# Four DRAM reads of each turn moved from the sync queue to ACT's queue in a two-layer decoder trunk

## The chip, the cores and the metric

One Trainium2 chip, one core. The metric is the device time of one execution of the program in microseconds (us). In the rows that follow, PE is the matmul engine (PEld its weight loads), DVE, ACT and POOL are the vector, scalar and general engines, and SP is the engine that issues most DMAs. An entry such as SPq or ACTq is a DMA issue on that engine's queue. L186 is line 186 of the kernel.

## What is computed

A trunk of two decoder layers over 256 positions of width 2048, all in float32. Cut to what matters:

```
for l in range(2):
    h = rmsnorm(x, attn_norm[l])
    z = h @ w_in[l]                     # q, k, v of four head groups, 4 heads x 128 each
    mixed = concat(fox(z), moba(z), diff(z), stick_breaking(z))
    x = x + mixed @ w_out[l]
    h = rmsnorm(x, ffn_norm[l])
    act = silu(h @ w_gate[l]) * (h @ w_up[l])        # width 5632
    x = x + act @ w_down[l]
return rmsnorm(x, final_norm)
```

## The kernel before

**Weights.** All weights are streamed once, in 784 blocks of 128 x 1024 numbers (512 KB). `load(b)` (L186, on SP) brings a block into one of four `raw` buffers. `split_parts` makes of it a rounded half `hi` on ACT (L195) and the rest `lo` on DVE (L196), each with three buffers. PE then multiplies a block by the activations with three products (hi by hi, hi by lo, lo by hi), twelve matmuls for each block (L356 to L358 in the projections, L374 in the gate and up products).

**The order of the work** is written out by hand: instructions stand on each engine's queue in the order in which the code issues them, and a queue doesn't overtake. For each block `run_ahead` issues the load of a block some way ahead, then `hi` and `lo` of the block three ahead of PE; then come the twelve matmuls, and then `tick()`, which moves three lists of generators (`evacs`, `background`, `spare`) one step on. So a generator's `yield` means: the next step stands one block later in every queue. Buffers tie the stream together: a `raw` buffer comes free when `lo` of its block is done, so `load` waits on DVE; a `hi` buffer comes free when PE is done with its block, so `hi` waits on PE.

**The turn.** Activations come out of PE with positions on the partitions; the next stage wants channels there. `turn_steps` (L379 to L397) does that through DRAM. DVE transposes 32 x 32 squares into `tr` (L384); one step later SP writes `tr` to the DRAM tile `mem` (L387); two steps later four reads of 128 KB each bring `mem` back with its parts rearranged (L393), each into 32 partitions, either into a tile `back` or straight into a `q` or `k` tile; two steps after that the consumer stands. There are 50 turns: 16 of q or k of the head groups, 22 of the FFN's activations (`act_steps`, L896 on ACT and L897 on DVE read `back`), and 12 of output columns (`add_turned`): four after each layer's output projection, and four after the first layer's down projection. In `add_turned`, DVE adds `back` to the residual `x_all` (L833); ACT and DVE make the next stage's operand `xh` of it (L299, L300), from which PE goes on. In a turn of q or k, ACT copies `back` (L429), or PE reads the tile itself (L612 and others).

Of the kernel before, what the change touches and what calls it, by code (L numbers as in the profile page):

```python
# [167 lines left out]
def trunk(ctx: ExitStack, tc: tile.TileContext, x_t, vec, w, consts, fin, y):  # L168
    nc = tc.nc
# [209 lines left out]
    def turn_steps(get, back=None):  # L379


        tr = tp.tile([P, 2, GC], F32, name="tr", tag="tr", bufs=1)
        for t in range(2):
            V.transpose(tr[:, t], get(t))  # L384
        yield
        mem = dr.tile([2, 4, 32, 4, P], F32, name="mem", tag="mem")
        nc.sync.dma_start(mem.rearrange("t i r g n -> (i r) t (g n)"), tr)  # L387
        yield
        yield
        if back is None:  # L390
            back = tp.tile([P, 8, 4, 32], F32, name="back", tag="back", bufs=1)
        for g in range(4):
            nc.sync.dma_start(back[32 * g:32 * g + 32].rearrange("r a k n -> r a (k n)"),  # L393
                              mem[:, :, :, g].rearrange("t i r n -> r (t i) n"))
        yield
        yield
        return back.rearrange("p a k n -> p k a n")  # L397
# [7 lines left out]
    def q_or_k_steps(name, which, outs, to, ready):  # L405

        z = tp.tile([P, 2, GC], F32, name="z", tag="g", bufs=1)
        if name in TABLES:
            at, n = TABLES[name]
            halves_of = lambda a: a.rearrange("p (s h n) -> p s h n", h=2, n=n)  # L410
            ms = tp.tile([P, 2, GC], F32, name="ms", tag="tr", bufs=1)
            for m, out in enumerate((z, ms)):
                for t in range(2):
                    tab = con[:, at + (2 * m + t) * n:at + (2 * m + t) * n + n]
                    V.scalar_tensor_tensor(out[:, t].rearrange("p (s n) -> p s n", n=n),
                                           outs[t].rearrange("p (s n) -> p s n", n=n), state["rcol"][:, t:t + 1],
                                           tab[:, None, :].to_broadcast([P, GC // n, n]), op0=ALU.mult, op1=ALU.mult)
            yield
            zh, mh = (a.rearrange("p t (s h n) -> p (t s) h n", h=2, n=n) for a in (z, ms))
            V.tensor_tensor(zh[:, :, 0], zh[:, :, 0], mh[:, :, 1], op=ALU.subtract)  # L420
            V.tensor_tensor(zh[:, :, 1], zh[:, :, 1], mh[:, :, 0], op=ALU.add)
        else:
            r = state["rq" if which == "q" else "rcol"]
            for t in range(2):
                A.activation(z[:, t], outs[t], AF.Copy, scale=r[:, t:t + 1])
        yield
        if which == STATIONARY[name]:
            new = yield from turn_steps(lambda t: z[:, t])
            A.activation(to.rearrange("p h (a n) -> p h a n", n=32), new, AF.Copy)  # L429
            yield  # L430
        else:
            yield from turn_steps(lambda t: z[:, t], to.rearrange("p h s -> p (h s)").rearrange("p (a h n) -> p a h n", h=NH, n=32))
        ready[which] = True
# [395 lines left out]
    def add_turned(n, outs, gain):  # L829

        new = yield from turn_steps(lambda t: outs[t])
        of = x_all[:, 4 * n:4 * n + 4].rearrange("p k (a n) -> p k a n", n=32)
        V.tensor_tensor(of, of, new, op=ALU.add)  # L833
        for j in range(4 * n, 4 * n + 4):
            halves_of_x(j, gain(j))
            square_sum(j)
            if j % 2:
                yield
# [168 lines left out]
```

## Time and profile before

| what | value |
| --- | --- |
| median of 3 runs | 2247.93 us |
| the runs | 2247.28 to 2248.83 us |
| the profiled execution | 2248.83 us |
| its span in the trace | 2247.0 us |
| mean granted TensorE clock | 0.996 of full speed |
| PE busy | 2223.6 us, 99% of the span |
| DVE busy | 1301.0 us, 58% |
| ACT busy | 1054.6 us, 47% |
| the sync queue's packets | 66.2% of the time of the 16 DMA engines |

The span is what the trace shows from the first instruction to the last; the profiled execution is 1.8 us longer, and itself 0.9 us above the median. Busy times leave out DMA issues, which the timeline shows as entries of SPq and ACTq. A timeline's row gives start, duration, engine, line, operation, output and inputs, the number of instructions run together, and in brackets the idle time just ahead of it with what ended it.

### The profile page before, as it was taken

The numbers are of one execution on the slowest core, as the hardware profiler recorded it, in microseconds if no ns is written. First come the engines' busy times: TensorE is split into PE (matmuls) and PEld (weight loads), VectorE is DVE, ScalarE is ACT, GpSimd is POOL, SyncE is SP. The second block draws the span as 40 slices with busy tenths as digits, with TensorE's granted clock in tenths as the row PEclk, the third lists the DMA queues.
The fourth block names the chain that finished last, engine by engine and source line by source line (L and its number), as shares of the span: only waits on it lengthen the run. The fifth ranks groups of instructions, "written<-read, shape, count | busy, mean of one in ns | idle before, by whom it ended". The sixth has DMA issues, their size and how long they took to land.

```text
span 2247.0 us, 26619 instructions
## 1 busy us (share of the span) xinstructions
PE 2223.6 (99%) x9977; PEld 1832.2 (82%) x9977; DVE 1301.0 (58%) x1442; ACT 1054.6 (47%) x1296; POOL 195.8 (9%) x189
## 2 busy tenths in 40 slices
PE   9999999999999999999999999999999999999997
PEld 6888888788888888888878888878888888888886
DVE  6768655655555555455566776566555555554444
ACT  6454644544444444444444556445444444444443
POOL 2019200100000000000000290011000000000000
PEclk9999999999999999999999999999999999999999
DMA  7766556777667667666657565567777776676664
GB/s 256 225 206 203 181 188 206 231 223 216 215 217 227 209 212 226 213 207 206 209 196 232 191 203 188 183 214 228 226 223 237 250 231 211 224 223 199 201 196 147
DMA packets 190497, 476.42 MB, mean 212 GB/s; under 512 B 17440, under 2 KB 72992, under 8 KB 190368
## 3 DMA queue, kind: packets, MB, share of 16 engines
q1 hardware_dynamic: 189792, 473.93, 66.2%
q8 instruction: 78, 1.28, 0.2%
q10 hardware_dynamic: 576, 0.79, 0.1%
q14 instruction: 51, 0.42, 0.1%
HBM read 444.24 MB, written 30.41 MB: 211 GB/s over the span
## 4 chain that ended last, share of the span: by engine, by line
PE 89%; DMA 4%; DVE 3%; ACT 2%; issue 1%; SPq 1%; ACTq 0%; DVEq 0%
PE gate L374 20%; PE up L374 20%; PE po L356 9%; PE po L358 9%; PE po L357 9%; PE in L356 7%; PE in L357 7%; PE in L358 7%; DMA back<-mem 2%; DMA mem<-tr 2%; DVE lo L196 1%; ACT hi L195 1%; SPq L393 0%; DVE x_all L833 0%; DVE tr L384 0%
## 5 line engine op out<-in xcount | busy, mean ns | idle before, releaser
L196 DVE TENSOR_TENSOR lo<-raw,hi 128x1024 fp32r<-128x1024 f32 (+1 forms) x785 | 961.2, 1227 | 880.1 <-ACT hi L195 879.6
L195 ACT ACTIVATE hi<-raw 128x1024 fp32r<-128x1024 f32 (+1 forms) x785 | 829.6, 1059 | 1080.3 <-PE up L374 487.4
L374 PE MATMUL gate<-hi,xh 128*128 128x512 f32 x1408 | 548.2, 389 | 0.5 <-ACT hi L195 0.5
L374 PE MATMUL up<-hi,xh 128*128 128x512 f32 x1408 | 547.8, 389 | 0.0
L374 PEld LDWEIGHTS gate<-hi,xh 128*128 128x128 f32 x1408 | 264.3, 188 | 56.0 <-ACT hi L195 1.2
L374 PEld LDWEIGHTS up<-hi,xh 128*128 128x128 f32 x1408 | 264.4, 188 | 54.8
L356 PE MATMUL in<-hi,xh 128*128 128x512 f32 x768 | 304.7, 397 | 4.1 <-ACT hi L195 2.3
L357 PE MATMUL in<-lo,xh 128*128 128x512 f32 x768 | 301.5, 393 | 1.4 <-DVE lo L196 1.3
L358 PE MATMUL in<-hi,xh 128*128 128x512 f32 x768 | 301.0, 392 | 0.0
L374 PE MATMUL gate<-lo,xh 128*128 128x512 f32 x704 | 274.5, 390 | 1.1 <-DVE lo L196 1.1
L374 PE MATMUL up<-lo,xh 128*128 128x512 f32 x704 | 273.9, 389 | 0.0
L356 PE MATMUL po<-hi,act 128*128 128x512 f32 x704 | 273.9, 389 | 0.0
L357 PE MATMUL po<-lo,act 128*128 128x512 f32 x704 | 273.9, 389 | 0.0
L358 PE MATMUL po<-hi,act 128*128 128x512 f32 x704 | 273.9, 389 | 0.0
L356 PEld LDWEIGHTS in<-hi,xh 128*128 128x128 f32 x768 | 145.4, 189 | 34.9 <-ACT hi L195 3.4
L357 PEld LDWEIGHTS in<-lo,xh 128*128 128x128 f32 x768 | 145.3, 189 | 32.5 <-DVE lo L196 3.3
L358 PEld LDWEIGHTS in<-hi,xh 128*128 128x128 f32 x768 | 145.3, 189 | 30.7
L374 PEld LDWEIGHTS gate<-lo,xh 128*128 128x128 f32 x704 | 132.1, 188 | 30.6 <-DVE lo L196 3.4
L358 PEld LDWEIGHTS po<-hi,act 128*128 128x128 f32 x704 | 132.2, 188 | 27.5
L357 PEld LDWEIGHTS po<-lo,act 128*128 128x128 f32 x704 | 132.2, 188 | 27.4
L356 PEld LDWEIGHTS po<-hi,act 128*128 128x128 f32 x704 | 132.2, 188 | 27.4
L374 PEld LDWEIGHTS up<-lo,xh 128*128 128x128 f32 x704 | 132.2, 188 | 27.2
(206 smaller groups left out, 1473.8 us busy)
## 6 DMA issues: line engine op xcount, KB each, us to landing
raw<-w SPq DMA_DIRECT2D x783, 512.0 KB, 4.3
mem<-tr SPq DMA_DIRECT2D x50, 512.0 KB, 4.3
back<-mem SPq DMA_DIRECT2D x168, 128.0 KB, 4.8
k<-mem SPq DMA_DIRECT2D x24, 128.0 KB, 4.2
memb<-trb SPq DMA_DIRECT2D x16, 128.0 KB, 3.8
x_all<-memb SPq DMA_DIRECT2D x4, 512.0 KB, 6.2
x_all<-x_t SPq DMA_DIRECT2D x7, 256.0 KB, 7.1
q<-mem SPq DMA_DIRECT2D x8, 128.0 KB, 4.7
```

Of the source, the lines that this page charges most:

```text
L195: A.activation(hi[:, c], raw[:, c], AF.Copy)
L196: V.tensor_tensor(lo[:, c], raw[:, c], hi[:, c].bitcast(F32), op=ALU.subtract)
L356: T.matmul(outs[t], xlo, wh, start=first, stop=False)
L357: T.matmul(outs[t], xhi, wl, start=False, stop=False)
L358: T.matmul(outs[t], xhi, wh, start=False, stop=last)
L374: T.matmul(outs[n][t], st, wt[:, n * GC:(n + 1) * GC], start=first, stop=last)
```

## The change

The four reads of `turn_steps` are issued by ACT (`nc.scalar`) and no more by SP (`nc.sync`). Where they stand among the steps, and the waits that they carry, are what they were.

```diff
@@ -390,7 +390,7 @@
         if back is None:
             back = tp.tile([P, 8, 4, 32], F32, name="back", tag="back", bufs=1)
         for g in range(4):
-            nc.sync.dma_start(back[32 * g:32 * g + 32].rearrange("r a k n -> r a (k n)"),
+            nc.scalar.dma_start(back[32 * g:32 * g + 32].rearrange("r a k n -> r a (k n)"),
                               mem[:, :, :, g].rearrange("t i r n -> r (t i) n"))
         yield
         yield
```

In all, 200 reads leave SP's queue and stand in ACT's; the orders of PE, DVE and POOL are what they were. ACT's queue at the third turn after the first layer's output projection (`hi130` is the rounded half of weight block 130, the number behind the name is the program's own):

```order
 L195 ACTIVATE hi128_3368<-raw128_3295 128x1024
 L195 ACTIVATE hi129_3386<-raw129_3325 128x1024
+L393 DMA back_3402<-mem_3364 32x8x128 x4
 L195 ACTIVATE hi130_3413<-raw130_3346 128x1024
 L195 ACTIVATE hi131_3431<-raw131_3366 128x1024
```

The four reads now stand between the halves of two neighbouring blocks, so `hi130` is behind whatever they wait for. SP's queue at the same place:

```order
 L186 DMA raw131_3366<-w 128x1024
 L186 DMA raw132_3384<-w 128x1024
-L393 DMA back_3402<-mem_3364 32x8x128 x4
 L186 DMA raw133_3411<-w 128x1024
 L186 DMA raw134_3429<-w 128x1024
```

The load of block 133 stood behind the reads; now it stands right behind the load of block 132. ACT's queue at a turn that goes straight into a `k` tile (layer 1, differential group):

```order
 L195 ACTIVATE hi422_9224<-raw422_9161 128x1024
 L195 ACTIVATE hi423_9242<-raw423_9181 128x1024
+L393 DMA k_8621<-mem_9220 32x8x128 x4
 L195 ACTIVATE hi424_9264<-raw424_9202 128x1024
 L195 ACTIVATE hi425_9282<-raw425_9222 128x1024
```

The pattern is the same one: the reads moved to behind `hi` of one block and ahead of `hi` of the next.

## Rows read from the trace of the kernel before

**Rows 1.** The page, busy us, share of the span and instructions by engine

```profile
PE 2223.6 (99%) x9977; PEld 1832.2 (82%) x9977; DVE 1301.0 (58%) x1442; ACT 1054.6 (47%) x1296; POOL 195.8 (9%) x189
```

**Rows 2.** Table by stretch: start:end, us, busy by engine, PEclk, DMA share, GB/s

```profile
345.00:450.00 105.00, 102.88 (x450) 83.35 (x449) 66.22 (x71) 53.38 (x75) 12.58 (x15) 1.00 0.70 220
450.00:900.00 450.00, 450.00 (x1987) 372.75 (x1986) 242.38 (x229) 199.26 (x208) 0.00 (x0) 1.00 0.70 218
900.00:1140.00 240.00, 238.45 (x1052) 197.17 (x1051) 126.95 (x115) 102.11 (x117) 9.26 (x11) 1.00 0.66 212
1140.00:1460.00 320.00, 318.39 (x1504) 262.69 (x1505) 210.97 (x292) 164.79 (x237) 74.75 (x66) 0.99 0.61 195
1460.00:1565.00 105.00, 103.35 (x452) 83.73 (x451) 65.78 (x71) 54.15 (x76) 12.60 (x15) 1.00 0.70 220
```

**Rows 3.** The page, DMA issues: KB of each, median us from issue to landing

```profile
mem<-tr SPq DMA_DIRECT2D x50, 512.0 KB, 4.3
back<-mem SPq DMA_DIRECT2D x168, 128.0 KB, 4.8
```

**Rows 4.** Waits: engine, line, what it waited for, us, times, longest

```profile
SPq L393 <- DMA mem<-tr: 25.2, 29, 2.4
...
ACT act L896 <- DMA back<-mem: 17.5, 12, 2.7
...
DVE x_all L833 <- DMA back<-mem: 10.9, 6, 2.5
```

**Rows 5.** Timeline of SP, third turn after the first output projection

```profile
397.07 0.38 SPq L387 DMA_DIRECT2D mem<-tr  x1
...
401.37 1.81 SPq L393 DMA_DIRECT2D back<-mem  x4
403.28 3.57 SPq L186 DMA_DIRECT2D raw<-w  x3
```

**Rows 6.** Timeline of ACT, the same turn

```profile
398.74 1.06 ACT L195 ACTIVATE hi<-raw 128x1024 fp32r<-128x1024 f32 x1 [1.87 <-PE po L358]
401.46 1.06 ACT L195 ACTIVATE hi<-raw 128x1024 fp32r<-128x1024 f32 x1 [1.66 <-PE po L358]
...
409.02 0.51 ACT L299 ACTIVATE xh<-x_all,vecs 128x256 fp32r<-128x256 f32 x1 [3.78 <-DVE x_all L833]
```

**Rows 7.** Timeline of DVE, the same turn

```profile
399.83 1.23 DVE L196 TENSOR_TENSOR lo<-raw,hi 128x1024 fp32r<-128x1024 f32 x1 [0.55 <-ACT hi L195]
...
407.76 1.23 DVE L833 TENSOR_TENSOR x_all<-x_all,back 128x1024 f32<-128x1024 f32 x1 [1.26 <-DMA back<-mem]
```

**Rows 8.** DMA issues from 403.25 to 403.6 us, with us to landing

```profile
raw<-w SPq DMA_DIRECT2D x1, 512.0 KB, 5.4
```

**Rows 9.** Table by stretch, columns as in rows 2, behind those reads

```profile
402.90:406.50 3.60, 3.60 (x18) 2.98 (x17) 2.10 (x2) 1.06 (x1) 0.00 (x0) 1.00 1.08 256
...
407.00:410.00 3.00, 3.00 (x15) 2.49 (x14) 1.66 (x2) 0.98 (x3) 0.02 (x1) 1.00 1.00 396
```

**Rows 10.** Pieces of the chain that ended last: start us, us, what

```profile
402.73 4.91 DMA back<-mem
...
1185.02 7.97 DMA back<-mem
```

**Rows 11.** Timeline of SP and DVE, last turn after the second output projection

```profile
1537.31 3.37 SPq L186 DMA_DIRECT2D raw<-w  x3
...
1542.23 1.23 DVE L833 TENSOR_TENSOR x_all<-x_all,back 128x1024 f32<-128x1024 f32 x1 [1.91 <-DMA back<-mem]
```

**Rows 12.** DMA issues from 1537.3 to 1537.6 us, with us to landing

```profile
raw<-w SPq DMA_DIRECT2D x1, 512.0 KB, 5.8
```

**Rows 13.** Timeline of PE, two places where it waited

```profile
392.98 0.50 PE L357 MATMUL po<-lo,mix 128*128 128x512 f32 x1 [0.66 <-DVE lo L196]
...
1214.52 0.68 PE L612 MATMUL s<-k,q 64*128 64x128 f32 x6 [0.23 <-DMA k<-mem]
```

**Rows 14.** Timeline of ACT, a DMA issue of its own at the end

```profile
2239.45 0.34 ACTq L977 DMA_DIRECT2D y<-x_all  x1
```

## The prediction

> **What bounds the kernel now.** I read the page's busy times first: PE works 99% of the span, ACT 47%, DVE 58% [rows 1]. So time can be won or lost only where PE stands still, and the table by stretch says where that is [rows 2]. From 450 to 900 us, the FFN of the first layer, PE doesn't idle at all. In the four other stretches shown it idles 105.00 - 102.88 = 2.12 us, 1.55, 1.61 and 1.65 us, together 6.93 us. These hold the two output projections (around 400 and 1515 us), the end of the down projection (1140 us) and the attention groups of the second layer. Next the chain that ended last: it leaves PE for a DMA piece of `back` at such places, as at 402.73 for 4.91 us and at 1185.02 for 7.97 us [rows 10]. At the output projections, DVE's add (L833) waits for the reads all in all 10.9 us, six times [rows 4], and ACT's `xh` waits for that add 3.78 us at 409.02 [rows 6]; `xh` stands ahead of the next `hi` and `lo`, and PE then waits for a `lo`, as at 392.98 for 0.66 us [rows 13]. So at these turns the landing of the reads sets PE's time, with next to no slack: a later landing is paid nearly one for one. In the FFN it is otherwise: ACT waits for the reads there up to 2.7 us (L896, twelve times) [rows 4], and PE doesn't idle [rows 2]. I take the 22 FFN turns as free for shifts of a microsecond.
>
> **Part 1: SP loses the 200 issues and the wait.** SP isn't a bound by its issue time, but what stands behind the reads matters. At the third turn the write of `mem` is issued at 397.07 and takes about 4.3 us to land [rows 3, 5]; SP waits for that, issues the four reads from 401.37 in 1.81 us, and only at 403.28 the next weight load [rows 5]. I call that load C. Its `raw` buffer was free when `lo` ended at 399.83 + 1.23 = 401.06 [rows 7]. With the reads gone, C is issued at 401.06, 2.22 us earlier and 0.3 us before the first read. SP's waits for `mem` fall away (25.2 us over 29 turns, 2.4 us at most [rows 4]), but that isn't a gain, since PE doesn't wait for these weights; it is the reason for which loads come earlier and meet the reads.
>
> **Part 2: ACT gains them.** One issue is 1.81 / 4 = 0.45 us on SP [rows 5]; ACT's own issue at the end of the kernel took 0.34 us [rows 14]. 200 x 0.45 = 90 us, beside some 1190 us in which ACT is idle [rows 1]. In order, though, the next `hi` stands behind them. At the third turn ACT comes to the reads with `hi` at 398.74, waits for `mem` until 401.37, and is free at 401.37 + 1.81 = 403.18 where the next `hi` started at 401.46 [rows 5, 6]: 1.7 us late. The cover: blocks follow each other every 401.46 - 398.74 = 2.72 us [rows 6]; `hi` starts when PE lets go of the block three back, so PE has two blocks, 5.44 us, before it needs the new one; `hi` takes 1.06 and `lo` 1.23 [rows 6, 7], which leaves 5.44 - 2.29 = 3.15 us. 1.7 is inside that: nothing. Without that cover each such turn would cost up to 1.7 us. The late `hi` makes the next `lo`, and with it the load behind C, later by the same 1.7 us.
>
> **Part 3: the reads meet C on the DMA engines.** This is the term that decides. No row shows reads of one queue beside loads of another in mid-kernel, so I bound it from both sides.
> - *Above:* all of C goes in front of the reads. Then they land no later than reads and C landed together before, since the bytes are the same: C landed at 403.28 + 5.4 = 408.68 [rows 5, 8], and the add started at 407.76 [rows 7]. That is 0.92 us. At the last such turn it is 1537.31 + 5.8 = 1543.11 against 1542.23, 0.88 us [rows 11, 12]. Worked out in the same way, the six adds of the two output projections give 0.88 to 1.11 us, 5.8 in all. Four more turns lie on the chain or close to it: two that go straight into `k` (of these, PE waits at 1214.52 for 0.23 us [rows 13]) with 0.9 each, the last column of the first down projection with 0.6, and a `q` turn at 1185 [rows 10] with 1.2. All of it: 9.4 us.
> - *Below:* the reads no longer stand in line behind loads issued just ahead of them and land earlier. More than PE's 6.93 us of idle time [rows 2] can't come back.
> - *Between:* from 402.9 to 406.5 us, while the reads were under way, the DMA engines' share was full (1.08) but they moved only 256 GB/s; with loads alone it is 396 GB/s [rows 9]. 256 GB/s x 3.6 us is 0.92 MB, of which the reads are 4 x 0.13 = 0.52; the other 0.40 MB were load bytes, so a good part of C and of the rest of its forerunner already went beside the reads. What the change can push ahead in addition is the rest of C, 0.52 - 0.40 = 0.12 MB, which at 396 GB/s is 0.3 us. Up to 0.9, if the 0.40 MB were mostly the forerunner's.
>
> The row of the same stretch is nearer to the case than the landing bound, so I take 0.4 us for the seven places where something waits for the reads already or PE follows closely (six adds and a `k` turn), and 0.2 us for the other three: 7 x 0.4 + 3 x 0.2 = 3.4 us.
>
> **The sum.** Part 1: 0; part 2: 0; part 3: +3.4. The profiled execution took 2248.83 us, span 2247.0; 2252.2 by it. It was 0.9 us above the median of its runs, so the forecast for a median is 2247.9 + 3.4 = 2251.3 us, +0.15%. A measurement of this kernel can tell about 0.2% (4.5 us) from no change, so this forecast is in the band of "the same", if near its upper end.
>
> **The rivals.**
> - *C goes wholly in front (slower).* The place: the ten turns of part 3. The price: 0.9 us each, 9.4 at most, say 8: 2256 us. For it: at 401.06 C is issued before the reads are, and the engines are full [rows 9]. Against it: the load behind C is 1.7 us later (part 2), so only one load can get in front. It decides from 0.5 us a turn, since ten turns at 0.5 are 5 us. The Trainium skill, "DMA: Bandwidth & Descriptors", Queues, rings and completion order, says that a DMA engine takes turns between the queues that have work for it, a whole packet at a time. By that rule C, now in the other queue, gets turns between the four reads, and the time would lie between the forecast and this rival.
> - *The reads land earlier (faster).* On their own queue they don't wait for loads ahead of them; the `q` turn whose reads took 7.97 us [rows 10] against 4.8 in the median [rows 3] is the best witness. If each of the ten turns got 0.7 us or more, most of the idle time comes back: some 5 of 6.93 us, 2243 us. Against it: at the third turn the last read's piece takes 4.91 us [rows 10], the median, so few loads can be ahead of it; and engines that are full [rows 9] aren't faster with two queues. The same page, section Issuing engines are not separate DMA queues, speaks against it: transfers issued from different engines share the same DMA engines.
> - *ACT in line (slower).* If an issue on ACT costs twice 0.45 us, or ACT reaches the reads only later, the next `hi` is later than the cover of 3.15 us (1.7 + 1.8 = 3.5), and each of the turns where ACT waits for `mem` costs PE 0.4 us and more; with the chain's ten turns at 1 us it is 2258 us. Against it: 0.34 us in the one row of ACT's own [rows 14]. The point from which it decides is 3.15 us of delay of one `hi`.
> - *The change doesn't do what it says:* the order shows that it does, at all 50 turns; no chance for that.
>
> **How the numbers follow.** Forecast (-1 to +4.5): 0.47. C in front: 0.36. Reads earlier: 0.10. ACT in line: 0.07. Slower by over 0.2%: the second and the last, less the part of C in front that stays below 0.5 us a turn: 0.36 + 0.07 - 0.01 = 0.42. The same: 0.47 + 0.01 = 0.48. Faster: 0.10. The range: down to 2245 us, which takes in small gains and half of the faster rival; up to 2258 us, past the 9.4 us of the upper bound (2257.3) and the nearest case of ACT in line. The forecast's own range is 2247 to 2252.4.
>
> **What would show it.** Right: C issued some 2 us earlier, at the end of `lo`; the wait of `hi` behind the reads 1 to 2 us longer with no new wait on PE; the waits of L833 for `back` up from 10.9 to some 13 us; PE idle in the two output projections up by 1 us each. Rival one: L833 starts at 408.6 and not 407.8, relative to its turn, and PE idles 2.5 us more in each output projection. Faster: the chain's `back` pieces shorter than 4.9 us, and the idle time of [rows 2] down. ACT in line: PE waits for `hi` or `lo` in the middle of an output projection, one or two blocks behind the reads, and in the FFN too. Wrong altogether: a change in the FFN stretches, where I count on nothing, or 200 issues that last longer on ACT than on SP.

## The result, and the profile after

The changed kernel took 2268.90 us (median of 3 runs, 2265.36 to 2269.46) against 2247.93 before: a ratio of 1.0082, 95% interval 1.0067 to 1.0097. It is slower by 21 us, where the prediction had +3.4 us and a range that ended at 2258. The profiled execution is the fastest of the three, 2265.36 us with a span of 2263.5, so the two traces differ by 16.5 us and not by 21.

The busy times of the page, answering to [rows 1], and the DMA queues, in which the reads now stand as q10:

```profile
PE 2227.7 (98%) x9977; PEld 1835.5 (81%) x9977; DVE 1303.4 (58%) x1442; ACT 1053.1 (47%) x1296; POOL 197.9 (9%) x189
...
q1 hardware_dynamic: 135392, 447.70, 60.6%
q10 hardware_dynamic: 54976, 27.02, 5.6%
```

PE's idle time, span less busy time, went from 2247.0 - 2223.6 = 23.4 us to 2263.5 - 2227.7 = 35.8 us. That is 12.4 of the 16.5 us. The other 4.1 us are PE's own: it was busy longer with the same number of instructions. The table by stretch, to be held against [rows 2]:

```profile
345.00:450.00 105.00, 97.75 (x420) 78.48 (x419) 62.77 (x69) 48.91 (x72) 12.51 (x15) 0.98 0.68 207
450.00:900.00 450.00, 450.00 (x1987) 372.92 (x1986) 243.27 (x231) 200.03 (x209) 0.00 (x0) 1.00 0.69 218
...
1460.00:1565.00 105.00, 99.06 (x431) 80.23 (x430) 61.43 (x64) 47.29 (x69) 12.47 (x15) 0.98 0.67 204
```

The FFN stretch is full, as it was. The two stretches with the output projections idle 7.25 and 5.94 us where they idled 2.12 and 1.65, and the granted clock in them is 0.98 and no more 1.00. Where the longest wait stands, it is lower still (the same view, a stretch behind the fourth turn):

```profile
435.00:442.00 7.00, 3.92 (x12) 2.60 (x11) 5.67 (x7) 5.77 (x11) 3.31 (x4) 0.81 0.19 62
```

PE worked 3.92 of these 7.00 us, and its granted clock was 0.81 of full speed on the mean, so some of the stretch was at the lower of its two levels. That accounts for PE's 4.1 busy microseconds in part at least. The mean granted clock of the whole run went from 0.996 to 0.994; an estimate from these means and the spans is 0.006 x 2263.5 - 0.004 x 2247.0 = 4.6 us of full-speed work, and since the means have three digits, it is good to some 2 us. So a wait costs more than itself.

What was waited for, us, times and longest, with the lines of [rows 4] again and PE's own:

```profile
ACT act L896 <- DMA back<-mem: 34.5, 19, 3.7
...
DVE x_all L833 <- DMA back<-mem: 18.1, 6, 4.1
...
PE gate L374 <- ACT hi L195: 5.9, 3, 2.6
PE s L612 <- DMA k<-mem: 3.8, 4, 1.3
```

The add in `x_all` waits for the reads 18.1 us where it waited 10.9, still six times, and PE waits for `k` itself 3.8 us where it was 0.2. SP's wait for `mem` ahead of the reads is gone, as foreseen. PE's wait for `hi` in the gate product was 0.5 us before; how it follows from the late add is shown with the third turn below.

The third turn after the first output projection, the one shown in [rows 5 to 7], as the timelines of SP, ACT, DVE and PE have it now:

```profile
398.68 0.38 SPq L387 DMA_DIRECT2D mem<-tr  x1
...
402.70 0.33 SPq L186 DMA_DIRECT2D raw<-w  x1
...
407.27 1.46 SPq L186 DMA_DIRECT2D raw<-w  x2
...
403.01 1.81 ACTq L393 DMA_DIRECT2D back<-mem  x4
404.92 2.01 ACT L195 ACTIVATE hi<-raw 128x1024 fp32r<-128x1024 f32 x2 [3.51 <-DMA raw<-w]
...
401.44 1.23 DVE L196 TENSOR_TENSOR lo<-raw,hi 128x1024 fp32r<-128x1024 f32 x1 [0.55 <-ACT hi L195]
...
411.93 1.22 DVE L833 TENSOR_TENSOR x_all<-x_all,back 128x1024 f32<-128x1024 f32 x1 [3.56 <-DMA back<-mem]
...
413.19 0.51 ACT L299 ACTIVATE xh<-x_all,vecs 128x256 fp32r<-128x256 f32 x1 [6.26 <-DVE x_all L833]
...
415.71 0.50 PE L374 MATMUL gate<-hi,xh 128*128 128x512 f32 x1 [1.80 <-ACT hi L195]
```

The last two rows are the path to PE: `xh` waits for the add and stands ahead of the next `hi` on ACT (414.62), and PE waits 1.80 us for that `hi`. Load C goes at 402.70, when `lo` has ended (401.44 + 1.23 = 402.67), 0.3 us before the first read. `hi` behind the reads starts at 404.92. From the issue of the write of `mem` to the add it is now 411.93 - 398.68 = 13.25 us; before it was 407.76 - 397.07 = 10.69 [rows 5, 7]. What the DMA engines did between (packets, MB, share of the engines, from 403.0 to 405.0 us and then from 406.5 to 411.0; ahead of them the issue of load C, with us to landing):

```profile
raw<-w SPq DMA_DIRECT2D x1, 512.0 KB, 6.5
...
q1 hardware_dynamic: 218, 0.81, 102.1%
...
back<-mem ACTq DMA_DIRECT2D x4, 128.0 KB, 7.2
```

```profile
q10 hardware_dynamic: 1002, 0.48, 67.0%
q1 hardware_dynamic: 150, 0.55, 48.9%
```

In the first two microseconds behind the reads' issue only loads moved, and up to 406.2 us no packet of q10 at all. C landed 6.5 us behind its issue, at 409.2. Nearly all of the reads (0.48 of 0.52 MB) moved in the 4.5 us from 406.5 on, beside 0.55 MB of loads, and each read landed 7.2 us behind its issue in the median, where the median of all was 4.8 in the kernel before [rows 3].

Over the six adds of the output projections that wait (second to fourth of each layer), the time from the issue of the write of `mem` to the start of the add, read off the timelines of SP and DVE as above, adds up to 68.1 us before and 79.2 after. That is 11 us more, 1 to 2.6 us a turn, against 16.5 us of the span; the `k` turns and the clock come on top. At the second `k` turn PE waits at 1222.41 and again at 1223.93 (timeline of PE), against 0.23 us at [rows 13]:

```profile
1222.41 0.46 PE L612 MATMUL s<-k,q 64*128 64x128 f32 x2 [1.34 <-DMA k<-mem]
1223.93 0.78 PE L612 MATMUL s<-k,q 64*128 64x128 f32 x6 [1.07 <-DMA k<-mem]
```

### The profile page after: what moved, and what is told of

Read it like the earlier page. It is cut to its first block, busy times and chain, and to the rows that moved or that the text cites. A ratio compares the mean times of both kernels' runs of the same rounds, so it can differ in the third digit from the quotient of the medians.

```text
span 2263.5 us, 26666 instructions
## 1 busy us (share of the span) xinstructions
PE 2227.7 (98%) x9977; PEld 1835.5 (81%) x9977; DVE 1303.4 (58%) x1442; ACT 1053.1 (47%) x1296; POOL 197.9 (9%) x189
## 4 chain that ended last, share of the span: by engine, by line
PE 88%; DMA 5%; DVE 3%; ACT 2%; issue 1%; ACTq 1%; SPq 0%; DVEq 0%
PE gate L374 20%; PE up L374 20%; PE po L356 9%; PE po L358 9%; PE po L357 9%; PE in L356 7%; PE in L357 6%; PE in L358 6%; DMA back<-mem 2%; DMA mem<-tr 2%; DVE lo L196 1%; ACT hi L195 1%; DMA raw<-w 1%; DMA k<-mem 1%; ACTq L393 1%
```

## The experiments

Three theories were put up. **1:** the loads that come in front of the reads make the loss, since SP is no longer held up. **2:** a queue of their own serves the reads worse beside the loads. **3:** ACT is blocked by the reads, and the next `hi` comes too late. Each run was timed beside the kernel before on the same chip; ratios are to that, with 95% intervals.

### ACT is blocked, the reads stay on SP

```diff
+        tiny = ...
+        for g in range(4):
+            nc.scalar.dma_start(tiny[32 * g:32 * g + 32], mem[0, 0, :, g, :1])
         for g in range(4):
             nc.sync.dma_start(back[...], mem[:, :, :, g]...)
```

> The reads stay on SP; on ACT, where the changed kernel has its reads, stand four reads of 128 bytes from the same DRAM tile, so ACT waits for the tile and issues four DMAs there, and the next hi is as late as in the changed kernel. Theory 3: 2260 to 2270 us. Theories 1 and 2: 2247 to 2250 us.

Measured: 2244.88 us (2242.70 to 2246.57), ratio 0.9982 (0.9972 to 0.9991). ACT, DVE and SP at its third turn:

```profile
398.42 1.84 ACTq L394 DMA_DIRECT2D tiny<-mem  x4
400.37 2.01 ACT L195 ACTIVATE hi<-raw 128x1024 fp32r<-128x1024 f32 x2 [3.58 <-issue]
...
405.10 1.23 DVE L836 TENSOR_TENSOR x_all<-x_all,back 128x1024 f32<-128x1024 f32 x1 [1.28 <-DMA back<-mem]
...
398.47 4.33 SPq L396 DMA_DIRECT2D back<-mem  x4
402.90 1.34 SPq L186 DMA_DIRECT2D raw<-w  x3
```

ACT stands for 3.58 us, as in the changed kernel (3.51), and `hi` is as late. No time is lost, and PE waits for `hi` 1.3 us in all, where it was 3.1 in the kernel before and 11.0 in the changed one: the cover that the prediction worked out (3.15 us beyond what is needed) holds. The edit did one thing more: SP's four reads took 4.33 us to issue and not 1.81, so load C went out 402.90 - 394.08 = 8.82 us behind the write of `mem`, where it was 403.28 - 397.07 = 6.21 [rows 5]. The total alone could therefore hide a cost under a gain; PE's waits for `hi` are what speaks against theory 3, and it falls by them.

### The reads on SP, behind load C

```diff
         yield
         yield
+        yield
         for g in range(4):
             nc.sync.dma_start(back[...], mem[:, :, :, g]...)
         yield
-        yield
```

> The reads stay on SP but stand one block later there, behind load C; their consumer stands where it was. Theory 1: C goes in front, in the same queue, and nothing that is issued later can pass: some 0.9 us for each of ten turns, 2254 to 2258 us; if C alone made the whole loss, 2264 to 2270. Theories 2 and 3: 2247 to 2250 us.

Measured: 2285.17 us (2279.31 to 2287.46), ratio 1.0154 (1.0133 to 1.0175): more than any theory had. SP at the second turn, and the add:

```profile
383.93 0.38 SPq L387 DMA_DIRECT2D mem<-tr  x1
385.04 3.20 SPq L186 DMA_DIRECT2D raw<-w  x3
388.30 3.04 SPq L394 DMA_DIRECT2D back<-mem  x4
...
397.78 1.23 DVE L833 TENSOR_TENSOR x_all<-x_all,back 128x1024 f32<-128x1024 f32 x1 [4.45 <-DMA back<-mem]
```

With C in front, in one and the same queue and with nothing of ACT's in it, `mem` to add is 397.78 - 383.93 = 13.85 us; over the six adds it is 77.5 us, close to the changed kernel's 79.2. So neither ACT nor a second queue is needed for the loss at these turns. Its 36 us in all are more than C's: the edit puts the reads a block later at all 50 turns, also where they didn't wait for `mem`, and the add then waits 12 times (30.8 us in all) and not six. The run separates theory 1 from 2 and 3 by its turns, and doesn't give the price of C by its total.

### Load C held back, first try

```diff
+        tiny = ...
-            nc.sync.dma_start(back[...], mem[:, :, :, g]...)
+            nc.scalar.dma_start(back[...], mem[:, :, :, g]...)
+        for g in range(4):
+            nc.sync.dma_start(tiny[32 * g:32 * g + 32], mem[0, 0, :, g, :1])
```

> The four reads are issued by ACT, as in the changed kernel; in their old place on SP stand four reads of 128 bytes each from the same DRAM tile, so SP waits for the tile as before and the next weight load (C) stays behind that wait. Theory 1 (loads in front: what costs the time is that C and the loads behind it are issued earlier than the reads): 2247 to 2252 us, close to the kernel before. Theory 2 (own queue: the reads are served worse on ACT's queue beside loads of the sync queue, whatever the order of issue): 2260 to 2270 us. Theory 3 (ACT in line: the next hi is held up behind the reads on ACT): 2260 to 2270 us too.

Measured: 2279.31 us (2277.56 to 2285.82), ratio 1.0138 (1.0116 to 1.0159). It looks like theory 2 or 3, but can't be counted for either. ACT at the second turn, and ACT's longest group of waits of this kind:

```profile
387.99 4.92 ACTq L394 DMA_DIRECT2D back<-mem  x4
393.03 2.00 ACT L195 ACTIVATE hi<-raw 128x1024 fp32r<-128x1024 f32 x2 [6.87 <-DMA back<-mem]
```

```profile
ACT hi L195 <- DMA tiny<-mem: 111.1, 23, 7.5
```

The issue of the four reads took 4.92 us and not 1.81. In the trace the landings are counted on eight semaphores, in nearly equal shares; that the four added DMAs on the other queue made reads wait for the landing of earlier ones on the same semaphore would fit, and isn't shown. ACT then stood 6.87 us, over twice the cover. The run changed something that it was not meant to change, so it doesn't separate the three theories.

### Load C held back until the reads have landed

On ACT's queue, and then the same on SP's:

```diff
+        tiny = ...
+            nc.scalar.dma_start(back[...], mem[:, :, :, g]...)     # first run; nc.sync in the second
+        nc.sync.dma_start(tiny[:1], back[96:97, 0, 0, :1])
```

> Reads on ACT as in the changed kernel; on SP a read of 4 bytes from the last part of what they bring stands in their old place, so no load behind it is issued until the reads have landed. Theory 1: the reads land as early as in the kernel before or earlier; the loads come some 6 us late, which the four buffers bear in part: 2244 to 2255 us, and if it is slower, by a wait of hi for its weights. Theory 2: the reads still land late, 2262 us or more.

> The same hold, but the reads on SP as in the kernel before. Theory 1: like the run with the reads on ACT and the hold, within 4 us of it. Theory 2: 10 us or more faster than that run.

Measured: 2243.19 us (2242.38 to 2244.23), ratio 0.9976 (0.9967 to 0.9986) with the reads on ACT, and 2242.82 us (2241.01 to 2245.50), ratio 0.9978 (0.9969 to 0.9987) on SP. Once no load is issued beside the reads, it makes no difference whose queue they stand in: a queue of their own is no loss by itself. What theory 2 says of loads issued right ahead of the reads is left to the next test. The third turn of the first:

```profile
405.25 0.59 SPq L396 DMA_DIRECT2D tiny<-back  x1
405.93 1.71 SPq L186 DMA_DIRECT2D raw<-w  x2
...
405.35 1.22 DVE L835 TENSOR_TENSOR x_all<-x_all,back 128x1024 f32<-128x1024 f32 x1 [0.16 <-DMA back<-mem]
```

C goes at 405.93, after the reads have landed, and the four buffers bear it.

### The bytes of C taken out of the way

The sharpest of the tests: all queues, waits and issues of the changed kernel, but C's first 64 columns alone at its early place and the other 960 behind the next load; then 512 and 512.

```diff
+        n = 64 if short[0] else 1024          # 512 in the second run; short[0] is set behind each turn's reads
-        nc.sync.dma_start(raws[b], w[b])
+        nc.sync.dma_start(raws[b][:, :n], w[b][:, :n])
+        ...                                   # the rest goes out behind the next load
```

> The changed kernel (reads on ACT), but load C, the first load behind each turn's reads, is issued at its early place with 64 of its 1024 columns, and its other 960 columns follow behind the next load. All waits, the queues and ACT's order are those of the changed kernel; only the bytes of C are no longer ahead of the reads. Theory 1 (load C's bytes in front of the reads make the loss): 2247 to 2254 us. Theory 2 (reads on a queue of their own are served worse beside the other queue, or land later for their issue by ACT): 2262 to 2270 us, as the changed kernel.

> As the run in which load C was issued early with 64 columns, now with 512 of its 1024, the other half behind the next load. If the loss goes with the bytes ahead of the reads: about half of it, 2253 to 2260 us. If it is the presence of a whole load (by the number of its pieces in line): near 2265. If the loss has a threshold (slack that half a load uses up): 2245 to 2250.

Measured: 2245.07 us (2242.72 to 2247.22), ratio 0.9991 (0.9982 to 1.0000) with 64 columns; 2254.24 us (2251.08 to 2257.11), ratio 1.0022 (1.0012 to 1.0032) with 512. The changed kernel once more, beside the second:

> The changed kernel once more, beside the runs that follow: 2265 to 2270 us.

Measured: 2270.53 us (2265.61 to 2271.46), ratio 1.0092 (1.0072 to 1.0113).

So with a sixteenth of C in front nothing is lost, with half of it 0.2%, with all of it 0.9%. The six adds go the same way: 68.8, 73.0 and 79.2 us from `mem` to add, where the kernel before has 68.1. (One trace's sum is good to some 3 us: it is 71.0 in the run, below, in which only the FFN's reads stand on ACT and these six turns are as before.) The third turn of the first of the two runs, ACT and DVE:

```profile
399.41 1.82 ACTq L402 DMA_DIRECT2D back<-mem  x4
401.33 2.07 ACT L204 ACTIVATE hi<-raw 128x1024 fp32r<-128x1024 f32 x2 [3.37 <-DMA raw<-w]
...
405.94 1.23 DVE L843 TENSOR_TENSOR x_all<-x_all,back 128x1024 f32<-128x1024 f32 x1 [1.17 <-DMA back<-mem]
```

From the first read to the add it is 405.94 - 399.41 = 6.53 us, as it was before (407.76 - 401.37 = 6.39 [rows 5, 7]), with ACT's queue, ACT's block of 3.37 us and the early issue all in place. In the changed kernel it is 411.93 - 403.01 = 8.92. Theory 1 stands, and theory 2 falls with it: the same queue beside the same earlier loads loses nothing, and in one queue (the run with the reads on SP behind C) the six adds lose as much. The loss grows faster than the bytes do.

The DMA engines in this run, in the first two microseconds from the reads' issue (399.4 to 401.4 us), and from 402.5 to 404.0, when the reads had them to themselves:

```profile
q1 hardware_dynamic: 215, 0.78, 99.1%
q10 hardware_dynamic: 4, 0.00, 0.3%
...
q10 hardware_dynamic: 576, 0.28, 111.9%
```

The first two microseconds belong to the sync queue here too, where nothing is lost; what moves then are loads issued ahead of C. The reads' first packet stands 1.9 us behind their first issue (401.3 us), with half of C in front 2.5 (405.5 against 403.01) and with all of it 3.2 (406.2 against 403.01). From the first packet to the add it is 4.6 us here and 5.7 in the changed kernel. So the 2.4 us between the two kernels at this turn part into a later start, 1.3, and a slower passage, 1.1.

### And load D?

C as in the changed kernel, but the load behind it with 64 columns in its place (the edit against the run with 64 columns of C; a count of one now cuts the load).

```diff
-        short[0] = 1      # the next load is cut
+        short[0] = 2      # the load after the next is cut
```

> The changed kernel, load C whole and early, but the load behind it (D) with 64 columns in its place and the other 960 behind the load after. The bound of the prediction said: reads and C land together no later than they did before, so at most 0.9 us a turn, if nothing else gets in. If D is what broke it: 2250 to 2257 us. If C alone makes the loss: 2262 to 2270 us.

Measured: 2263.25 us (2259.30 to 2274.91), ratio 1.0058 (1.0035 to 1.0081). C alone makes a loss of 15 us in the median, by the interval of the ratio 8 to 18; D may add some 7 us (2270.5 - 2263.3), but the two intervals overlap, and the runs of this kernel lie far apart. D's share is left open.

### Which turns

> Only the 22 turns of the FFN have their reads on ACT; the other 28 stay on SP. If the loss sits in the turns ahead of which PE has no cover (output projections, k turns), as the prediction said: 2247 to 2250 us. If the FFN's turns carry a part by way of the granted clock or a later stage: 2252 us or more.

> Only the 12 turns of output columns have their reads on ACT. By the shifts read from the trace of the changed kernel, the output projections make 11 of its 17 us and two k turns the rest: 2257 to 2262 us.

The edit is one argument to `turn_steps`, which names the queue. With the 22 FFN turns on ACT: 2249.61 us (2245.28 to 2253.01), ratio 1.0000 (0.9990 to 1.0009). ACT's wait for the reads grows there, and PE doesn't notice (waits, and the table by stretch, of this run):

```profile
ACT act L896 <- DMA back<-mem: 41.8, 20, 5.2
```

```profile
450.00:900.00 450.00, 450.00 (x1987) 372.59 (x1987) 242.89 (x230) 198.71 (x209) 0.00 (x0) 1.00 0.70 219
```

With the 12 turns of `add_turned` alone: 2262.06 us (2259.14 to 2263.44), ratio 1.0057 (1.0038 to 1.0077), so 14 of the 22 us. That leaves the rest to the turns of `q` and `k`, if the shares add up; they were not run alone.

### The other way round: the reads in front of load B

If what stands in front of the reads sets their landing, it should pay to put them a block earlier on SP, ahead of B too.

```diff
         yield
-        yield
         for g in range(4):
             nc.sync.dma_start(back[...], mem[:, :, :, g]...)
         yield
         yield
+        yield
```

> Reads on SP, one block earlier in its order: ahead of the load that stood in front of them too (B). If what goes ahead of the reads sets their landing (theory 1), they land about 1 to 2 us earlier at the ten turns and the load B comes some 4 us late inside the cover: 2242 to 2247 us; if B's lateness is more than the cover, PE waits for hi and lo and it is 2250 to 2265 us. Theory 2 says nothing of it.

Measured: 2238.31 us (2237.38 to 2239.61), ratio 0.9957 (0.9941 to 0.9974): faster than both kernels. SP and DVE at the third turn, and the reads in the list of DMA issues:

```profile
394.39 0.38 SPq L387 DMA_DIRECT2D mem<-tr  x1
395.50 0.33 SPq L186 DMA_DIRECT2D raw<-w  x1
398.65 1.81 SPq L392 DMA_DIRECT2D back<-mem  x4
400.57 4.16 SPq L186 DMA_DIRECT2D raw<-w  x4
...
404.29 1.22 DVE L833 TENSOR_TENSOR x_all<-x_all,back 128x1024 f32<-128x1024 f32 x1
```

```profile
back<-mem SPq DMA_DIRECT2D x168, 128.0 KB, 3.1
```

Three loads were in front of the reads in the changed kernel (A, B, C), two before, one here, and a read lands in 5.7, 4.8 and 3.1 us in the median of all turns. `mem` to add is 404.29 - 394.39 = 9.90 us, with no wait for the reads any more: now the `lo` ahead of it on DVE sets its start.

## Why the prediction was wrong

**The place was right.** The FFN turns cost nothing; the output projections and the `k` turns pay, six adds and two `k` turns, as named. The last column of the first down projection, also named, doesn't in the trace: 12.27 us from `mem` to add before, 12.26 after; nor does the `q` turn, where ACT's wait for the reads is 3.03 us before and 2.58 after. C is issued at the end of `lo`, 0.3 us before the first read, as worked out.

**Part 2 was right.** `hi` is late behind the reads by the amount foreseen (an idle of 3.51 us ahead of it, where it was 1.66 and 1.7 were to be added) and PE has cover for it; the run with ACT blocked and the reads on SP shows it, and so does the one with 64 columns. The rival "ACT in line" has fallen.

**Part 3 failed, in its upper bound.** It said that reads and C together land no later than they did before, since the bytes are the same, so C in front costs at most some 0.9 us a turn and 9.4 in all. At the third turn the add came 8.92 us behind the first read's issue and not 6.39: 2.5 us later, where the bound gave 0.92. In all it is 21 us; with all of C in front and D out of the way still some 15 in the median (2263.3 against 2248.4), though the interval of that run, 8 to 18, reaches down to the bound. The signs say the same: L833 waits 18.1 us where the forecast had 13, and the two output projections idle 5.1 and 4.3 us more where the forecast had 1 each and the rival 2.5. By the bound, reads and C should have been there 408.68 - 401.37 = 7.31 us behind the first read's issue, at 410.32 in the changed kernel. C was, at 409.2; the reads were used at 411.93, 1.6 us too late. So the same bytes took longer in the other order, and that is what "since the bytes are the same" had left out.

The traces show where. The reads' first packet stood 3.2 us behind the issue, where it was 1.9 with C's bytes away, and from there to the add it took 5.7 us, where it was 4.6; D's bytes were beside them at the end. Why they start so late isn't shown: from 405.4 to 406.2 us only the sync queue moved, 0.18 MB at a share of 68.0%, so the engines weren't full while the reads waited. The prediction had also taken the share of 1.08 of [rows 9] for engines that are full, and reckoned in bytes from there. A share says little of bytes: the reads alone moved 0.28 MB in 1.5 us, 184 GB/s, at 111.9%, and loads alone 396 GB/s at 1.00 [rows 9]. With hindsight, the rival "C goes wholly in front" was the nearer one, but at a price of its own: C's own time at 396 GB/s (0.52 MB, 1.3 us) on each of ten turns would be 13 us, 2261 us. That is an estimate, and still short of the 2268.90 measured.

**The value between the bounds** was then taken from the wrong side. The 0.3 us came from the bytes that "already went beside", in the order of issue before, in which C stood behind the reads; beside or behind them is not the same as ahead of them. The dose (64, 512, 1024 columns in front: none, 0.2%, 0.9%) shows that it is the bytes ahead that count.

**Rule and row.** Of the Trainium skill, "DMA: Bandwidth & Descriptors", Queues, rings and completion order, I had used the rule that a DMA engine takes turns between queues, by which the reads would have got theirs between C's packets. Once both have packets under way, the trace agrees: from 406.2 to 407.2 us, before D is issued (407.27) and when the loads issued ahead of C had landed (the later one at 400.92 + 4.8 = 405.7), C's packets on q1 and the reads' on q10 moved side by side:

```profile
q10 hardware_dynamic: 329, 0.16, 62.4%
q1 hardware_dynamic: 47, 0.16, 47.0%
```

What I had made of the rule failed all the same: the reads' turns didn't begin at their issue but 3.2 us later, and the time came out beyond the rival and not between it and the forecast.

**What was left out:** the waits bring the granted clock down (0.98 in the two stretches, 0.81 in one piece of 7 us), and PE's own busy time grew by 4.1 us. No term of the sum stood for that. The same term had the limit of the faster rival too low. In the run with the reads ahead of load B, PE's line is

```profile
PE 2219.0 (99%) x9977; PEld 1832.7 (82%) x9977; DVE 1300.0 (58%) x1442; ACT 1053.5 (47%) x1296; POOL 198.1 (9%) x189
```

Its busy time is 4.6 us less than before [rows 1], and the gain of 9.6 us is more than the 6.93 us of idle time which, by the prediction, was all that could come back.

**The faster rival** had a grain of truth, turned round: the reads can land earlier, by standing in front of load B on SP, not by a queue of their own.

## What to carry to other kernels

A queue's blocking wait may be doing work: here it held big loads back until small, urgent reads were out, and taking the reads off the queue set the loads free to go first. Ask of every DMA that is moved what stood behind it, when that now starts, and whether it lands in front of something that is waited for. A DMA share near one doesn't say how many bytes move: look at the GB/s beside it, and don't take it that the same bytes take the same time in another order.

## What was not expected of the hardware

Reads of 128 KB in small pieces, four in a row, took 6.4 us from first issue to use at one turn with two 512 KB loads ahead of them, 8.9 with three; in the run with one ahead each landed in 3.1 us in the median. On a queue of their own they had their first packet 1.9 us behind the issue with a sixteenth of the third load ahead, and 3.2 with all of it. And the loss isn't proportional to the bytes in front: half a load cost 0.2%, a whole one 0.9%.
